# Storing the transposed X and Z from ScalarE's queue, with a third place for the transposed X

## The chip, the cores and the metric

The kernel runs on one core of a Trainium2 chip. Its engines are TensorE (PE in the profile, with its weight loads as PEld), VectorE (DVE), ScalarE (ACT), GpSimd (POOL) and SyncE (SP), which here only issues transfers. All engines work side by side, each in its own fixed order, and meet at semaphores. The metric is the device time of one execution in microseconds (us), as the median of several runs.

## The reference

One inference step of one layer: 512 latent tokens and 128 context tokens of width 2048 go through adaLN modulation, an input projection, a time mixer (RWKV-7, scanned in both directions, 16 heads of 64) beside a chunked gMLP, an output projection and a SwiGLU channel mixer. The part that matters here is the scan:

```python
def step(S, inp):
    r_t, w_t, k_t, v_t, a_t, b_t = inp
    sa = jnp.einsum('bhvk,bhk->bhv', S, a_t)
    S = S * w_t[:, :, None, :] + sa[..., None] * b_t[:, :, None, :] + v_t[..., None] * k_t[:, :, None, :]
    return S, jnp.einsum('bhvk,bhk->bhv', S, r_t)

h = _rmsnorm(x, lp['norm1_g']) * (1.0 + sc1) + sh1
p = h @ lp['w_in']
o_a, s_fin = _rwkv7_bidir(shift_fn(p[..., :C_SHIFT], lp['mu_shift']), s0, lp)
```

All arrays are float32.

## The kernel before

All 640 tokens are kept together, in 10 chunks of 64 (`NCH`, `CH`). The scan is done chunk by chunk in matrix form. It has two stages. In the first, while the input projection runs on TensorE, the operands of every chunk are prepared and stored in a DRAM array `d_S`, one record for each head pair, direction and chunk. In the second stage, the records are read back and the states are carried from chunk to chunk.

**The stage around the change.** The loop over `pieces` runs the input projection: 128 output columns at a time (a block), in four pieces of 512 rows of `w_in`. `split` (L160) loads a piece of weights through SP's queue into one of three buffers `raw`, ACT makes the rounded part `hi` (L167), VectorE the remainder `lo` (L168), and `win` (L183) does three products with them into two halves of a PSUM tile `big`. Weights are loaded two pieces ahead (`LEAD`). A finished block is copied out by ACT (`praw`, L952) and handed to a function for its kind of column: `take_r`, `take_v`, `take_k`, `take_gv`, `take_gu`. These are generators; between the matmuls of `win` the three mixers `mixA`, `mixS` and `mixM` run a bit of them at a time, each `yield` naming a cost. So the program interleaves the projection with the preparation of the scan. The 1 MB loads of `w_mod` (`wt`, L889), with the products `pm` (L900), are strewn in as well. A planner then lays out the order of each engine from estimated times of the instructions and from their dependencies; it also puts in the semaphores. The transfers issued by SP and by ACT share a set of eight semaphores in turn, so a transfer may first wait for an earlier one that used the same semaphore.

**The lines that the change touches** are in `take_k`, which runs once for each of the 8 head pairs and in it twice, once a direction: 16 times, each called a half-pair here. For one half-pair it does the following in this order.

- It makes the decay factors, then R (stored at L622) and X, a tile of 10 chunks. Two loads from `d_vt` (L626) put the values into two blocks of each chunk of the tile Z.
- The products `pG` (L650) give GR (stored at L664, six stores), GA and GB.
- The transposes `pXT` (L668) turn X: first chunks 0 to 7, then chunks 8 and 9, each for two heads h into two PSUM banks. So there are four copies of a PSUM bank into a tile XT by ACT (L674): two of 128x512 and two of 128x128 elements. XT has two places. Each copy is followed by a store to `d_S` (L676): two of 256 KB and two of 64 KB.
- The products `pW` (L682) use the same two PSUM banks, so each bank must have been copied to XT before. ACT copies the four results into the free blocks of Z (L684), and one store of 640 KB brings Z to `d_S` (L686).
- The small blocks of GB go out through GpSimd's queue for the next step, `solve`, and then `merge`, which `mixS` and `mixM` run.

SP's queue is in order: a store at L676 or L686 waits there for ACT's copy, with all later loads and stores behind it. ACT issues only a few transfers: five at the start and, in the second stage, the new states (L1205).

Of the kernel before, what the change touches and what calls it, by code (L numbers as in the profile page):

```python
# [10 lines left out]
F32 = mybir.dt.float32  # L11
# [8 lines left out]
P = 128  # L20
# [5 lines left out]
CH = 64  # L26
# [18 lines left out]
SDIV = 9.0  # L45
HOLD = 68
WAIT = 20
SUBST = 4.6
MODR = 1.36
NREC = 8  # L50
# [34 lines left out]
F_R, F_G, F_X, F_Z, F_T, REC = 0, 128, 256, 384, 512, 576  # L85
# [3 lines left out]
def flow_step(ctx: ExitStack, tc, x_prompt, x_sample, state_rwkv, c, c_ctx, w_mod, b_mod,  # L89
# [3 lines left out]
    nc = tc.nc  # L93
# [59 lines left out]
    d_S = dp.tile([NPAIR, P, 2, NCH, REC], F32, name="d_S")  # L153
# [207 lines left out]
    bk, bp, gs, bz = (hp.enter_context(tc.tile_pool(name=n, bufs=1)) for n in ("bk", "bp", "gs", "bz"))  # L361
# [138 lines left out]
    def both(name):  # L500
        return [pk.tile([P, 512], F32, tag=f"g{h}", name=name) for h in range(2)]

    def in_turn(fns):
        last = None
        for fn in fns:
            if last is None:
                last = fn()
            else:
                with tc.issue_after(last.ins):
                    last = fn()  # L510
# [38 lines left out]
    def take_k(pr, p):  # L549
# [30 lines left out]
        for d in range(2):  # L580
# [5 lines left out]
            for hf in range(2):  # L586
# [6 lines left out]
                for h, dst in enumerate((sg, tha)):  # L593
                    c = 16 * h + 8 * d + p
# [28 lines left out]
            Z = bz.tile([P, NCH, 2, CH], F32, tag="Z", name="Z")  # L623
# [42 lines left out]
            for (c0, c1) in ((0, 8), (8, NCH)):  # L666
                two = [ps.rearrange("p (c t) -> p c t", t=CH) for ps in both("pXT")]
                in_turn([lambda cc=cc, h=h: TE.transpose(  # L668
                    two[h][:, cc - c0, :], X[hsl(h), cc].rearrange("p s t -> p (s t)"), ident[hsl(h), hsl(h)])
                    for cc in range(c0, c1) for h in range(2)])  # L670
                for h in range(2):
                    ps = two[h]
                    XT = bz.tile([P, 8, CH], F32, tag="XT", name="XT", bufs=2)
                    S.copy(XT[:, 0:c1 - c0, :], ps[:, 0:c1 - c0, :])  # L674
                    yield 0.1 * (c1 - c0)
                    nc.sync.dma_start(d_S[p, :, d, c0:c1, F_X + CH * h:F_X + CH * h + CH], XT[:, 0:c1 - c0, :])  # L676
            two = [ps.rearrange("p (c t) -> p c t", t=CH) for ps in both("pW0")]
            for c0 in (0, 5):
                ps = two[c0 // 5][:, 0:5, :]
# [3 lines left out]
                for h in range(2):  # L683
                    S.copy(Z[osl(h), c0:c0 + 5, h, :], ps[osl(h)])  # L684
                yield 1.0
            nc.sync.dma_start(d_S[p, :, d, :, F_Z:F_Z + P], Z.rearrange("p c h v -> p c (h v)"))  # L686
            o.dd[d] = db.tile([8, NCH, 16, 16], F32, tag=f"dd{d}", name="dd")
            for gq in range(8):
                q = gq % 4
# [99 lines left out]
    def solve(p):  # L789
# [4 lines left out]
        for d in range(2):  # L794
            BQ.dma_start(gi[:, d], o.dd[d].rearrange("g c s t -> g c (s t)"))
        yield WAIT
        tc.keep_in_program_order(V.memset(mx2[:, :, 0], 0.0))
# [128 lines left out]
    for p in range(NPAIR):  # L926
        block(P * p, take_r, 2.6, p)
        block(2 * DA + P * p, take_v, 5.1, p)
        block(DA + P * p, take_k, KCOST, p)
        while g < GORD[p]:  # L930
            block(CSH + DA + P * g, take_gv, 12.0, g)
            block(CSH + P * g, take_gu, 5.0, g)
            g += 1
# [21 lines left out]
    def between(k):  # L955
        if k in GRAN:
            f = 1.0 / (2 * len(GRAN))
            mixA.run(f * max(AMIN, 8.0 * mixA.pace()))
            mixS.run(f * SUBST)
            mixM.run(f * max(SMIN, mixM.left / SDIV), k == GRAN[-1])  # L960
# [1158 lines left out]
```

## Time and profile before

| what | us |
|---|---|
| median of 3 runs | 3245.55 |
| range of the runs | 3244.21 to 3252.82 |
| the profiled execution: its time | 3255.98 |
| the profiled execution: its span | 3254.2 |

The span runs from the first to the last instruction of the program; 1.8 us of the profiled execution's time lie outside it. The views used are these. Busy time counts work of an engine; issuing a transfer and waiting for a semaphore are not counted as busy. A row of the waits names who waited, for whom, the total in us, the number of times and (in the list of all waits) the longest. A row of the groups has a line, an engine, an operation, the tiles written and read, the count, busy time and mean duration in ns, and the idle time of the engine ahead of them with what ended it. A row in order of time has a start, a duration and, in brackets, the idle time ahead of it with what ended it. SP's own rows end in q, since all that it does is done by its sequencer; so do ACT's issues. The list by line has the shortest, the median and the longest duration in ns. In the chain of waits, a row that begins with DMA is the time from the issue of a transfer to the wait that it ended.

### The profile page before, as it was taken

What the parts mean: (1) busy time and instruction counts of PE and PEld (TensorE: products, weight loads), DVE (VectorE), ACT (ScalarE), POOL (GpSimd) and SP (SyncE); (2) the same over time, 40 slices, a digit from 0 to 9 for tenths busy, and PEclk for the clock granted to TensorE, in tenths of its full rate; (3) what the DMA queues carried; (4) which work ended last, traced back from release to release, by engine and by line L of the source; (5) the groups of instructions that cost most, each with busy time, mean ns of one, the idle gap of its engine ahead of it and who ended that gap; (6) DMA issues with size and microseconds to landing.
All of it is one profiled execution on the core that took longest, in us unless ns stands there. A gap on an engine that the chain in (4) does not pass through costs nothing.

```text
span 3254.2 us, 72319 instructions
## 1 busy us (share of the span) xinstructions
PE 3113.8 (96%) x28216; PEld 2872.8 (88%) x28216; DVE 2365.7 (73%) x4115; ACT 1459.9 (45%) x3197; POOL 1218.3 (37%) x1065
## 2 busy tenths in 40 slices
PE   6999999999999999999999999999999999999997
PEld 3687778777777888899899999999999999999997
DVE  4548766676676677766878778777777787887788
ACT  3344444454344444345644444444444445443365
POOL 2001121211112113422356655665665645454542
PEclk9999999999999999999999999999999999999999
DMA  9666676777678588654444344344344364553453
GB/s 371 222 197 197 192 217 181 197 205 193 184 194 227 159 275 269 200 173 151 129 130 122 106 129 127 103 128 127 108 124 121 117 189 150 162 155 105 150 165 120
DMA packets 740438, 550.88 MB, mean 169 GB/s; under 512 B 141056, under 2 KB 673504, under 8 KB 731264
## 3 DMA queue, kind: packets, MB, share of 16 engines
q1 hardware_dynamic: 727136, 532.47, 54.2%
q0 software_dynamic: 10624, 13.23, 1.8%
q8 instruction: 222, 3.64, 0.5%
q14 instruction: 120, 0.98, 0.1%
q10 hardware_dynamic: 2336, 0.57, 0.1%
HBM read 437.79 MB, written 110.95 MB: 169 GB/s over the span
## 4 chain that ended last, share of the span: by engine, by line
PE 72%; DVE 10%; DMA 7%; issue 6%; POOL 3%; ACT 2%; SPq 0%; DVEq 0%; POOLq 0%; ACTq 0%
PE P L1637 15%; PE P L1635 15%; PE P L1636 15%; PE big L189 5%; PE big L191 4%; PE big L190 4%; PE pm L900 2%; DMA wt<-in_w_mod_dram 1%; DVE lo L1417 1%; PE pG L650 1%; PE big L1475 1%; PE big L1476 1%; PE big L1477 1%; PE big L1032 1%; DVE mx L803 1%
## 5 line engine op out<-in xcount | busy, mean ns | idle before, releaser
L1637 PE MATMUL P<-xo,lo 128*128 128x320 f32 x2352 | 728.0, 310 | 2.6 <-DVE lo L1417 2.5
L1635 PE MATMUL P<-xo,hi 128*128 128x320 f32 x2352 | 727.4, 309 | 0.7 <-ACT hi L1416 0.7
L1636 PE MATMUL P<-xo,hi 128*128 128x320 f32 x2352 | 727.2, 309 | 0.0
L1417 DVE TENSOR_TENSOR lo<-raw,hi 128x512 fp32r<-128x512 f32 x526 | 499.9, 954 | 178.0 <-ACT hi L1416 172.8
L1416 ACT CAST hi<-raw 128x512 fp32r<-128x512 f32 x526 | 327.0, 622 | 486.0 <-PE P L1636 384.6
L189 PE MATMUL big<-h_hi,hi 128*128 128x320 f32 x1376 | 450.9, 328 | 8.2 <-ACT hi L167 4.8
L1637 PEld LDWEIGHTS P<-xo,lo 128*128 128x128 f32 x2352 | 441.9, 188 | 4.0 <-DVE lo L1417 4.0
L1635 PEld LDWEIGHTS P<-xo,hi 128*128 128x128 f32 x2352 | 441.9, 188 | 1.0 <-ACT hi L1416 1.0
L1636 PEld LDWEIGHTS P<-xo,hi 128*128 128x128 f32 x2352 | 441.9, 188 | 0.0
L191 PE MATMUL big<-h_hi,lo 128*128 128x320 f32 x1376 | 434.2, 316 | 1.1 <-DVE lo L168 0.9
L190 PE MATMUL big<-h_lo,hi 128*128 128x320 f32 x1376 | 433.6, 315 | 0.6 <-DVE h_lo L351 0.6
L1545 POOL TENSOR_TENSOR raw<-raw 128x512 f32<-128x512 f32 x252 | 409.0, 1633 | 16.4 <-DVE lo L1417 4.9
L1637 PE MATMUL P<-xd,lo 128*128 128x320 f32 x1232 | 385.2, 313 | 18.7 <-DVE lo L1417 18.4
L1635 PE MATMUL P<-xd,hi 128*128 128x320 f32 x1232 | 383.1, 311 | 1.5 <-ACT hi L1416 0.6
L1636 PE MATMUL P<-xd,hi 128*128 128x320 f32 x1232 | 382.1, 310 | 0.0
L168 DVE TENSOR_TENSOR lo<-raw,hi 128x512 fp32r<-128x512 f32 x268 | 184.0, 689 | 204.0 <-ACT hi L167 193.6
L189 PEld LDWEIGHTS big<-h_hi,hi 128*128 128x128 f32 x1376 | 262.5, 191 | 76.2 <-issue 50.6
L1416 ACT CAST hi<-rawd 128x512 fp32r<-128x512 f32 (+1 forms) x288 | 168.8, 587 | 243.5 <-PE P L1636 206.4
L191 PEld LDWEIGHTS big<-h_hi,lo 128*128 128x128 f32 x1376 | 262.6, 191 | 10.8 <-issue 3.5
L190 PEld LDWEIGHTS big<-h_lo,hi 128*128 128x128 f32 x1376 | 263.3, 191 | 6.4 <-issue 1.7
L167 ACT CAST hi<-raw 128x512 fp32r<-128x512 f32 x268 | 165.1, 618 | 223.9 <-PE big L190 112.2
L1637 PEld LDWEIGHTS P<-xd,lo 128*128 128x128 f32 x1232 | 232.5, 189 | 25.6 <-DVE lo L1417 25.4
(403 smaller groups left out, 6109.2 us busy)
## 6 DMA issues: line engine op xcount, KB each, us to landing
wt<-in_w_mod_dram SPq DMA_DIRECT2D x96, 1024.0 KB
raw<-in_w_ffn_gate_dram SPq DMA_DIRECT2D x182, 256.0 KB
raw<-in_w_ffn_up_dram SPq DMA_DIRECT2D x182, 256.0 KB
rec<-d_S SPq DMA_DIRECT2D x80, 576.0 KB
raw<-in_w_in_dram SPq DMA_DIRECT2D x172, 256.0 KB
rawd<-in_w_ffn_down_dram SPq DMA_DIRECT2D x128, 256.0 KB
raw<-in_w_out_dram SPq DMA_DIRECT2D x96, 256.0 KB
xd<-d_os SPq DMA_DIRECT2D x66, 320.0 KB
```

The source lines that it names most:

```text
L167: S.copy(hi, raw)
L168: V.tensor_sub(lo, raw, hi.bitcast(F32))
L189: TE.matmul(halves[hf], hi[:, k, :], h_hi[:, kb, s], start=(kb == 0), stop=False)
L190: TE.matmul(halves[hf], hi[:, k, :], h_lo[:, kb, s], start=False, stop=False)
L191: TE.matmul(halves[hf], lo[:, k, :], h_hi[:, kb, s], start=False, stop=(kb == KB - 1))
L900: TE.matmul(pm[32 * j:32 * j + 2, :], cT[:, 2 * kb:2 * kb + 2], quad[:, j, :], start=(kb == 0), stop=(kb == KB - 1), tile_position=(0, 32 ...
L1416: S.copy(hi[:, 0:nk], raw[:, 0:nk])
L1417: V.tensor_sub(lo[:, 0:nk], raw[:, 0:nk], hi[:, 0:nk].bitcast(F32))
L1545: G.tensor_tensor(out=o[:, 0:nk], in0=p[:, 0:nk], in1=q[:, 0:nk], op=ALU.subtract)
L1635: TE.matmul(ps, hi[:, k, :], xk[:, 0, :], start=f, stop=False)
L1636: TE.matmul(ps, hi[:, k, :], xk[:, 1, :], start=False, stop=False)
L1637: TE.matmul(ps, lo[:, k, :], xk[:, 0, :], start=False, stop=l)
```

## The change

The stores of XT and of Z are issued by ACT instead of SP, and XT has three places instead of two. A constant `NW` is added, which nothing uses.

```diff
@@ -45,6 +45,7 @@
 SDIV = 9.0
 HOLD = 68
 WAIT = 20
+NW = 8
 SUBST = 4.6
@@ -670,10 +671,10 @@
                 for h in range(2):
                     ps = two[h]
-                    XT = bz.tile([P, 8, CH], F32, tag="XT", name="XT", bufs=2)
+                    XT = bz.tile([P, 8, CH], F32, tag="XT", name="XT", bufs=3)
                     S.copy(XT[:, 0:c1 - c0, :], ps[:, 0:c1 - c0, :])
                     yield 0.1 * (c1 - c0)
-                    nc.sync.dma_start(d_S[p, :, d, c0:c1, F_X + CH * h:F_X + CH * h + CH], XT[:, 0:c1 - c0, :])
+                    nc.scalar.dma_start(d_S[p, :, d, c0:c1, F_X + CH * h:F_X + CH * h + CH], XT[:, 0:c1 - c0, :])
@@ -683,7 +684,7 @@
                 for h in range(2):
                     S.copy(Z[osl(h), c0:c0 + 5, h, :], ps[osl(h)])
                 yield 1.0
-            nc.sync.dma_start(d_S[p, :, d, :, F_Z:F_Z + P], Z.rearrange("p c h v -> p c (h v)"))
+            nc.scalar.dma_start(d_S[p, :, d, :, F_Z:F_Z + P], Z.rearrange("p c h v -> p c (h v)"))
```

A third place is 2 KB more in each partition of on-chip memory.

## The prediction

> **What bounds the kernel now.** I read the page first, then the busy time in four stretches, then who waited for whom in the one stretch in which the touched lines run, then single stalls in order of time.
>
> ```profile
> span 3254.2 us, 72319 instructions
> PE 3113.8 (96%) x28216; PEld 2872.8 (88%) x28216; DVE 2365.7 (73%) x4115; ACT 1459.9 (45%) x3197; POOL 1218.3 (37%) x1065
> PE 72%; DVE 10%; DMA 7%; issue 6%; POOL 3%; ACT 2%; SPq 0%; DVEq 0%; POOLq 0%; ACTq 0%
> ```
> ```profile
> 0.00:200.00 200.00, 165.59 (x1071) 122.27 (x1072) 95.12 (x207) 70.59 (x113) 19.56 (x37) 0.95 0.79 274
> 200.00:1050.00 850.00, 806.22 (x9477) 669.17 (x9477) 591.65 (x1141) 385.59 (x846) 149.85 (x245) 0.97 0.72 199
> 1050.00:1500.00 450.00, 432.34 (x6127) 386.74 (x6126) 318.47 (x843) 197.84 (x669) 113.14 (x142) 0.99 0.69 213
> 1500.00:3254.20 1754.20, 1709.62 (x11547) 1694.65 (x11545) 1360.49 (x1927) 805.83 (x1569) 935.71 (x642) 0.99 0.43 132
> ```
>
> The columns after the stretch are its length and the busy time of PE, PEld, DVE, ACT and POOL. TensorE sets the time. The edit touches only the stretch from 200 to 1050 us, where the 16 half-pairs (8 head pairs, two directions) are prepared. There TensorE stands idle for 850 - 806.2 = 43.8 us, and ACT is busy for 385.6, or 45%. So the edit can save at most a part of 43.8 us, and what it puts on ACT costs only where TensorE already stands waiting for ACT. The next view says which part that is.
>
> ```profile
> ACT XT L674 <- DMA d_S<-XT: 24.1, 7, 5.9
> ACT hi L167 <- DMA raw<-in_w_in_dram: 11.7, 13, 2.6
> PEld pW L682 <- ACT XT L674: 8.5, 5, 4.8
> PE pW L682 <- ACT XT L674: 7.2, 3, 4.5
> PE pm L900 <- DMA wt<-in_w_mod_dram: 5.5, 4, 2.7
> PEld pXT L668 <- ACT XT L674: 4.6, 12, 1.6
> ```
> ```profile
> L674 ACT COPY XT<-pXT 128x128 f32<-128x128 f32 x32 | 8.3, 260 | 24.6 <-DMA d_S<-XT 24.1
> ```
>
> Total, number, longest. ACT waits 24.1 us, 7 times, for a place of XT to come free, always at the small copies, which are the third and the fourth of a half-pair (the row by shapes); in order of time it is the third each time. TensorE itself waits for XT copies 7.2 us at the product pW, in three places. Weight loads overlap running matmuls, so the matmul rows count. One half-pair in order of time (ACT rows, then the three stalls of TensorE and one product after it):
>
> ```profile
> 640.91 1.06 ACT L674 COPY XT<-pXT 128x512 f32<-128x512 f32 x2
> 647.88 0.27 ACT L674 COPY XT<-pXT 128x128 f32<-128x128 f32 x1 [5.91 <-DMA d_S<-XT]
> 649.80 0.26 ACT L674 COPY XT<-pXT 128x128 f32<-128x128 f32 x1
> 648.20 0.80 PE L682 MATMUL pW<-Z,GA 64*64 64x64 f32 x20 [0.84 <-ACT XT L674]
> 684.95 0.80 PE L682 MATMUL pW<-Z,GA 64*64 64x64 f32 x20 [1.89 <-ACT XT L674]
> 934.59 1.33 PE L682 MATMUL pW<-Z,GA 64*64 64x64 f32 x20 [4.51 <-ACT XT L674]
> 937.48 1.33 PE L682 MATMUL pW<-Z,GA 64*64 64x64 f32 x20
> ```
>
> Copies 1 and 2 fill the two places; copy 3 comes when the first store has landed, here 6 us later; then pW can take its bank. 0.84 + 1.89 + 4.51 = 7.24, the whole of the row above.
>
> How much does ACT's standing still cost TensorE? I cut out the seven waits of copy 3 exactly (first, longest, and their sum):
>
> ```profile
> 231.33:234.91 3.58, 3.58 (x26) 3.46 (x26) 0.69 (x1) 0.00 (x1) 0.15 (x1) 1.00 1.06 295
> 641.97:647.88 5.91, 5.39 (x36) 4.87 (x35) 0.00 (x0) 0.01 (x1) 0.23 (x1) 1.00 0.86 240
> sum 24.14, PE 23.16 PEld 19.70 DVE 1.09 ACT 0.02 POOL 2.27; mean PE 3.31 PEld 2.81 DVE 0.16 ACT 0.00 POOL 0.32
> ```
>
> While ACT does nothing for 24.14 us, TensorE is busy for 23.16. A microsecond in which ACT stands costs 0.98 / 24.14 = 0.04 us of TensorE's time. That ratio limits both the gain and the loss.
>
> **The change, part by part.** The stores and what they cost on the queue that has them now:
>
> ```profile
> L676 SPq DMA_DIRECT2D d_S<-XT x64: 359/363/1603, 230.3 to 1027.4; - x64
> L676 SPq EVENT_SEMAPHORE  x55: 17/17/17, 229.1 to 1025.1; - x55
> L686 SPq DMA_DIRECT2D d_S<-Z x16: 359/363/1275, 240.2 to 1030.1; - x16
> L1205 ACTq DMA_DIRECT2D out_dram<-ST x8: 378/417/476, 1182.8 to 1389.5; - x8
> SPq L676 <- ACT XT L674: 64.4, 36, 6.4
> SPq L686 <- ACT Z L684: 20.4, 12, 4.0
> SPq L166 <- DVE lo L168: 212.6, 107, 8.8
> ```
>
> *Issues moved to ACT.* 64 + 16 = 80 issues leave SyncE (SP) and go to ACT, at 0.363 us there; the one store that ACT issues already (L1205) takes 0.417. Does an issue hold ACT's engine? The only place that shows it:
>
> ```profile
> 1182.77 0.44 ACTq L1205 DMA_DIRECT2D out_dram<-ST  x1
> 1182.82 0.19 ACT L1132 ACTIVATION_READ_ACCUMULATOR Y<-y_ps 128x1 f32 x1
> 1182.92 0.21 ACT L1132 ACTIVATE Y<-y_ps 128x64 f32<-128x64 f32 x1
> ```
>
> Here ACT went on computing beside the issue, because that store waits for VectorE. The stores of XT and Z wait for ACT's own copy, so nothing of ACT is left in flight and the next copy begins only after the issue. I take 0.42 us of standing for each, 80 x 0.42 = 33.6 us in all, on an engine that is idle 55% of the stretch. Exposed at the ratio of 0.04 that is 1.3 us. The lower bound is 0 (all issues fall in idle time). The upper one: behind a store stand the second copy of each pair, for which the transposes of the last chunks wait (12 times the weight load already stands there, 4.6 us), the fourth copy, for which the second pW waits, and after Z the next evacuation: 3 x 16 x 0.42 = 20 us. I take +2, near the row of the ratio.
>
> *Waits moved to ACT.* Ahead of 55 of the 64 XT stores, SP carries a further wait for an earlier transfer that uses the same semaphore. All lasted 17 ns, so they were over when SP came; on ACT I put 0 for them. Were one not over, the casts of weights (hi) and all evacuations would queue behind it.
>
> *Waits and issues off SP.* SP loses 80 x 0.363 = 29 us of issues (at the median) and 64.4 + 20.4 = 84.8 us of standing for ACT's copies, which held the weight loads behind them. But the loads mostly wait for a free buffer (212.6 us), and TensorE has no stall for them among its matmul rows except 5.5 us for wt. The longest of these, 2.7 us, ended with a load that took 9.26 us to land, so it was a late landing and not a late issue:
>
> ```profile
> 836.86 9.26 DMA wt<-in_w_mod_dram
> ```
>
> Bounds -5.5 and 0; a load let go earlier can also run into the stores, which the landing rows would show and no row prices. I take -0.5.
>
> *The third place.* It removes the wait of copy 3 for the first store. Copy 4 then waits for that store, where it now waits for the second. So the 24.1 us do not vanish: part moves to copy 4. The first pW is freed (-7.24 at best); the second pW, which now follows 2.9 us after the first (934.59 and 937.48), may stall in its place. In the 4.51 and the 1.89 us stalls copy 3 stood behind other ACT work, and copy 4 could come to stand there. Bounds -7.2 and 0; I take the middle, -4, for want of a row that decides.
>
> How late the first store lands decides what copy 4 still waits:
>
> ```profile
> 641.51 6.27 DMA d_S<-XT
> ```
>
> In the kernel before, 6.27 us from issue to release in the worst case, in one ring with 256 KB and 1 MB loads. The Trainium skill, page "DMA: Bandwidth & Descriptors", section "Queues, rings and completion order", says that a DMA engine takes the queues that have work in turn, packet by packet; by that the store would overtake SP's loads and copy 4 would wait hardly at all, and the third place would give its full -7.2. The same page's section "Issuing engines are not separate DMA queues" says that issuing from several engines saves only the sequencer's time to issue; by that the landing stays as it is and the sum would be that of my middle value or worse. No row of the kernel before decides between them.
>
> *Order.* A planner lays out each engine's order from estimated times, so work beside the stores can change places. Nothing in the trace prices that. The stretch has 43.8 / 16 = 2.7 us of idle TensorE time in a half-pair; I let a quarter of all of it, 11 us, come or go for the range.
>
> Sum: +2 + 0 - 0.5 - 4 = -2.5 us, against the profiled span of 3254.2. The unprofiled median is 3245.55, and the difference carries over: 3243. A difference under 0.3%, 9.7 us, I call no change; that is about what three runs, 3244.21 to 3252.82, can tell.
>
> **Rivals.** *Slower: issues between the copies.* Each store put between two evacuations makes TensorE wait for the second: the 20 us of the upper bound, less at most 4 from the third place, +16: 3262. For it: TensorE's weight loads already stand at these copies 12 times. Against it: the seven windows, in which ACT stood far longer than 0.42 us and TensorE lost 4%. It decides if the planner puts the issue ahead of the second copy, and if the slack at these points is under 0.42 us. Chance 0.17.
>
> *Faster: stores land early on their own ring.* Neither copy 3 nor copy 4 waits: -7.2, and SP, freed of 84.8 us, brings wt in time: -5.5, with issues hidden: -12.7, 3233. For it: the 6.27 us landing behind loads. Against it: it needs every stall of both rows to go, and the wt stalls are not at an XT store. Chance 0.15.
>
> *Nothing: the wait only moves.* Copy 4 takes copy 3's wait, the second pW the first one's stall, and the third place gives 0: +2 - 0.5, 3247. Chance 0.18.
>
> **How the numbers follow.** The forecast, 3243, has 0.50. With reordering of 11 us either way its own range is 3232 to 3254. The slower rival draws the upper end to 3258; at the lower end 3232 holds the faster one. About 0.1 is left out on each side. Faster by over 0.3%: the 0.15 and a little of the forecast's edge, 0.18. Slower: 0.17 and the same, 0.18. Within 0.3%: 0.64.
>
> **What would show it.** In the changed profile: 80 issues of about 0.4 us on ACT and none on SP; the wait of XT for its store far below 24.1 us, or moved to the fourth copy; pW's wait for XT copies (7.2) at 3 or less; the second transposes' wait for XT copies up by less than 3 us; TensorE's idle time of 43.8 us in the stretch changed by under 10. The slower rival shows as more idle time before pXT and pW that XT copies end, the faster one as the loss of both that and the wt wait. I am wrong if issues on ACT last over 1 us, if a semaphore wait ahead of them lasts microseconds, or if the stretches after 1050 us change.

## The result, and the profile after

| what | before | after |
|---|---|---|
| median, four runs each (us) | 3245.10 | 3273.65 |
| range of the runs (us) | 3244.21 to 3252.82 | 3267.75 to 3277.16 |
| the profiled execution: time (us) | 3255.98 | 3267.75 |
| the profiled execution: span (us) | 3254.2 | 3266.0 |

The change makes the kernel slower: ratio 1.0081 [1.0060, 1.0102] (in brackets the 95% interval). The two profiled executions show only 11.8 us of the 28.5 us between the medians, because the one of before was slower than all four of its kernel's runs and the one of after is the fastest of its four. All lines of the changed kernel from the copy of XT on bear a number one higher.

The page of the changed kernel: the span, the busy time of the engines, ACT's transfer queue (packets, MB, share of 16 engines) and the shares of the chain that ended last.

```profile
span 3266.0 us, 72293 instructions
...
PE 3108.7 (95%) x28216; PEld 2864.2 (88%) x28216; DVE 2358.8 (72%) x4115; ACT 1463.9 (45%) x3197; POOL 1225.1 (38%) x1065
...
q10 hardware_dynamic: 65056, 21.54, 2.6%
...
PE 69%; DVE 11%; DMA 8%; issue 6%; ACT 3%; POOL 3%; SPq 0%; ACTq 0%; DVEq 0%; POOLq 0%
```

TensorE is busy for no longer than before (3113.8 there), so the time was lost as idle time. ACT's queue carries 21.54 MB, where it carried 0.57. The four stretches, with the columns of before (PE, PEld, DVE, ACT, POOL, then the granted clock):

```profile
0.00:200.00 200.00, 165.87 (x1077) 122.14 (x1078) 96.23 (x207) 70.72 (x113) 19.55 (x37) 0.94 0.79 274
200.00:1050.00 850.00, 784.72 (x9163) 646.96 (x9161) 569.08 (x1111) 379.46 (x827) 145.38 (x241) 0.97 0.70 193
1050.00:1500.00 450.00, 431.22 (x6302) 383.45 (x6302) 319.54 (x845) 194.47 (x665) 113.04 (x143) 0.99 0.72 218
1500.00:3266.00 1766.00, 1726.90 (x11680) 1711.61 (x11678) 1373.93 (x1955) 819.23 (x1594) 947.10 (x646) 1.00 0.44 133
```

In the stretch with the stores TensorE stands idle for 850 - 784.72 = 65.3 us, 21.5 more than the 43.8 of before, at the same granted clock (0.97). It does 9163 products there instead of 9477; the others slip into the later stretches, so in the last one TensorE is busy for 17.3 us longer (1726.90 against 1709.62). The line of the XT stores, and the waits from 200 to 1080 us (total, times, longest; the last row is of before):

```profile
L677 ACTq DMA_DIRECT2D d_S<-XT x64: 366/427/1736, 229.8 to 1039.4; - x64
L677 ACTq EVENT_SEMAPHORE  x56: 17/17/17, 230.3 to 1039.4; - x56
```
```profile
ACT XT L675 <- DMA d_S<-XT: 45.2, 14, 5.5
PEld pW L683 <- ACT XT L675: 9.5, 8, 2.5
PE pW L683 <- ACT XT L675: 8.3, 7, 2.4
PE pm L901 <- DMA wt<-in_w_mod_dram: 14.8, 7, 5.5
PE pG L651 <- DVE GA L661: 12.0, 10, 2.6
```
```profile
PE pG L650 <- DVE GA L660: 3.4, 5, 1.4
```

All 64 stores are on ACT, at 0.427 us in the median, and the semaphore waits ahead of 56 of them were over when ACT came (17 ns each). But ACT now waits for a place of XT 14 times and 45.2 us in all, where it waited 7 times and 24.1 us. pW's wait for the copies of XT rose only from 7.2 to 8.3. Most of the 21.5 us is elsewhere: the wait of the products pm for wt rose from 5.5 to 14.8, and that of the products pG for GA, which VectorE writes, from 3.4 to 12.0.

One half-pair of the changed kernel in order of time, ACT, then the two products pW, then the first store in the chain of waits:

```profile
652.56 1.07 ACT L675 COPY XT<-pXT 128x512 f32<-128x512 f32 x2
653.17 1.27 ACTq L677 DMA_DIRECT2D d_S<-XT  x2
655.82 0.27 ACT L675 COPY XT<-pXT 128x128 f32<-128x128 f32 x1 [2.19 <-PE pXT L669]
660.77 0.27 ACT L675 COPY XT<-pXT 128x128 f32<-128x128 f32 x1 [4.68 <-DMA d_S<-XT]
660.85 0.89 ACTq L677 DMA_DIRECT2D d_S<-XT  x2
661.83 0.42 ACT L685 COPY Z<-pW 64x320 f32<-64x320 f32 x1 [0.80 <-ACT XT L675]
```
```profile
659.19 0.80 PE L683 MATMUL pW<-Z,GA 64*64 64x64 f32 x20
661.09 0.80 PE L683 MATMUL pW<-Z,GA 64*64 64x64 f32 x20 [1.10 <-ACT XT L675]
```
```profile
653.17 7.51 DMA d_S<-XT
```

Copy 3 gets the third place as soon as its transposes are done (655.82). Copy 4 follows it directly in ACT's order and stands for 4.68 us, until the first store has landed, 7.51 us after its issue (the row of the chain). Stores 3 and 4 are both issued behind copy 4, and Z's first copy begins when their issues are over. In the kernel before, ACT had other work in this place. I counted in both traces what ACT runs between the copies of the 16 half-pairs: before, 0 to 6 other instructions between copies 2 and 3 and 1 to 4 between 3 and 4; after, none in any of the 16. So the planner, which laid other work into the time of the landing in the kernel before, lays none there in the changed one.

The 14 waits cut out exactly (first, longest, and the sum of all):

```profile
231.46:236.95 5.49, 3.73 (x41) 3.41 (x39) 0.00 (x0) 0.00 (x0) 0.55 (x1) 1.00 1.04 289
...
821.20:826.61 5.41, 3.37 (x37) 2.99 (x37) 0.64 (x2) 0.01 (x2) 0.54 (x1) 1.00 0.89 238
...
sum 45.16, PE 37.98 PEld 31.62 DVE 4.65 ACT 0.02 POOL 5.39; mean PE 2.71 PEld 2.26 DVE 0.33 ACT 0.00 POOL 0.39
```

TensorE stands for 45.16 - 37.98 = 7.2 us of them, 16%, against 4% of the seven waits of before. The single waits are no longer (45.16 / 14 = 3.2 us in the mean, against 24.14 / 7 = 3.4), but TensorE ran out of work in seven of the 14, where it did so in two of the seven. What is held up on ACT behind the wait comes on top of that and isn't in these windows.

### The profile page after: what moved, and what is told of

Its sections match the earlier page's. It is cut to its first block, busy times and chain, and to the rows that moved or that the text cites. A ratio compares the mean times of both kernels' runs of the same rounds, so it can differ in the third digit from the quotient of the medians.

```text
span 3266.0 us, 72293 instructions
## 1 busy us (share of the span) xinstructions
PE 3108.7 (95%) x28216; PEld 2864.2 (88%) x28216; DVE 2358.8 (72%) x4115; ACT 1463.9 (45%) x3197; POOL 1225.1 (38%) x1065
## 3 DMA queue, kind: packets, MB, share of 16 engines
q10 hardware_dynamic: 65056, 21.54, 2.6%
## 4 chain that ended last, share of the span: by engine, by line
PE 69%; DVE 11%; DMA 8%; issue 6%; ACT 3%; POOL 3%; SPq 0%; ACTq 0%; DVEq 0%; POOLq 0%
PE P L1638 15%; PE P L1636 15%; PE P L1637 15%; PE big L190 4%; PE big L192 3%; PE big L191 3%; DMA wt<-in_w_mod_dram 2%; DMA d_S<-GR 2%; DVE lo L1418 1%; PE pm L901 1%; DMA d_S<-XT 1%; DVE mx L804 1%; PE big L1476 1%; PE big L1478 1%; PE big L1477 1%
```

## The experiments

Two causes lie in one edit: the stores go another way, and the planner lays a new order, in which, by the names in the profile, 462 of ACT's 3197 instructions and 3319 of TensorE's 28216 stand at another place, all of them behind the first store of XT. So beside the parts of the change there are kernels in which only a number that the planner's interleaving reads is altered. In the expectations of e1 to e12, A is the theory that ACT's queue holds up ACT, B that the planner's new order costs the time, C that transfers land late. Ratios are to the kernel before in the same series, with their 95% intervals.

**The parts one by one.** In e1 only the third place, in e2 only XT's stores on ACT, in e3 only Z's, in e4 both with two places.

```diff
-XT = bz.tile([P, 8, CH], F32, tag="XT", name="XT", bufs=2)
+XT = bz.tile([P, 8, CH], F32, tag="XT", name="XT", bufs=3)
```
```diff
-nc.sync.dma_start(d_S[p, :, d, c0:c1, F_X + CH * h:F_X + CH * h + CH], XT[:, 0:c1 - c0, :])
+nc.scalar.dma_start(d_S[p, :, d, c0:c1, F_X + CH * h:F_X + CH * h + CH], XT[:, 0:c1 - c0, :])
```
```diff
-nc.sync.dma_start(d_S[p, :, d, :, F_Z:F_Z + P], Z.rearrange("p c h v -> p c (h v)"))
+nc.scalar.dma_start(d_S[p, :, d, :, F_Z:F_Z + P], Z.rearrange("p c h v -> p c (h v)"))
```

The first block is e1, the second e2, the third e3, the second and third together e4.

> Both stores stay on SP, XT has three places. Three theories stand. (A) ScalarE's queue: in the changed kernel ACT stood 45.2 us at the fourth copy, with everything behind it, and the stores on ACT make this worse; the third place alone is then harmless or good, 3238 to 3246. (B) The planner's order: any edit that changes an estimated time lays out TensorE's order anew, and the +28 us are where the stalls happened to fall; then this edit too moves the time, by up to 20 us and with either sign. (C) Transfers: XT stores on ACT's queue land later (the first of a half-pair after 5.1 us on the mean instead of 4.1) and hold SP by the shared semaphores, so that wt comes late; nothing of it happens here: 3241 to 3249, and the wait of pm for wt stays near 5.5 us.

> XT's stores alone go to ACT, with two places as before; Z's store stays on SP. (A) 64 of the 80 issues are on ACT and the third copy waits in ACT's queue: most of the loss is here, 3262 to 3275. (B) Anything from 3235 to 3275, with no tie to the wait of ACT at XT. (C) Most of the loss is here, with the wait of pm for wt at 10 us or more.

> Z's store alone goes to ACT: 16 issues of 0.37 us. (A) At most 16 x 0.37 = 6 us: 3245 to 3251. (B) Not tied to that bound: 3235 to 3275. (C) Z's stores are few; 3243 to 3249, wt wait near 5.5 us.

> Both stores on ACT, XT with two places: the whole change without the third place. (A) As slow as the changed kernel or slower, 3268 to 3285, with ACT's wait for XT at 45 us or more. (B) Unrelated to the sum of the parts. (C) As slow as the changed kernel, 3265 to 3280, the wait of pm for wt at about 15 us.

| kernel | median us | ratio |
|---|---|---|
| e1, third place, SP's queue | 3253.27 | 1.0028 [1.0015, 1.0041] |
| e2, XT on ACT, two places | 3276.75 | 1.0091 [1.0075, 1.0107] |
| e3, Z on ACT | 3258.77 | 1.0043 [1.0027, 1.0059] |
| e4, both on ACT, two places | 3265.51 | 1.0065 [1.0053, 1.0077] |

Waits of e1, then of e2, then of e4:

```profile
ACT XT L674 <- DMA d_S<-XT: 2.9, 2, 1.8
PE pW L682 <- ACT XT L674: 0.6, 1, 0.6
```
```profile
ACT XT L674 <- DMA d_S<-XT: 43.7, 17, 7.3
PE pW L682 <- ACT XT L674: 11.1, 9, 2.3
```
```profile
ACT XT L674 <- DMA d_S<-XT: 53.8, 19, 7.7
PE pW L682 <- ACT XT L674: 13.9, 9, 3.7
```

The third place does on SP's queue what the change was thought to do: ACT's wait falls from 24.1 to 2.9 us, pW's from 7.2 to 0.6. Yet the kernel is slower. The move to ACT's queue does the reverse: with two places ACT waits 43.7 us in e2 and 53.8 in e4, at copy 3 in 30 of the 36 cases, where the six kernels with two places on SP's queue have 18.2 to 29.5. So it is the move that lengthened the wait; in the change the third place took 53.8 - 45.2 = 8.6 us off it again, and the wait now stands at copy 4. In e2 and e4 ACT has 1 to 3 other instructions between copies 3 and 4, by my count, so the copies stand close together only with the stores on ACT and three places or more. e3 lies above what A allowed (3251). Every part costs, and they don't add up (e2 alone costs more than e4, which holds it; their mean granted clocks are 0.982 and 0.985). So something other than the stalls at XT moves the time by ten microseconds.

**The planner's order alone, and four places.** e5 to e7 and e12 leave the stores as they are; each alters one number of the program's interleaving. e8 is the change with four places.

```diff
# e5
-yield 0.1 * (c1 - c0)
+yield 0.11 * (c1 - c0)
# e6
-WAIT = 20
+WAIT = 21
# e7, after the copies of Z
-yield 1.0
+yield 1.05
# e12
-KCOST = 50.0
+KCOST = 50.5
# e8, with both stores on ACT
-XT = bz.tile([P, 8, CH], F32, tag="XT", name="XT", bufs=3)
+XT = bz.tile([P, 8, CH], F32, tag="XT", name="XT", bufs=4)
```

> Nothing of the stores is changed: SP's queue, two places. Only the cost named by the yield after a copy of XT goes from 0.1 to 0.11 a chunk, which shifts a little what the program interleaves and so what the planner lays out. (A) and (C), the cost lies in what ACT and the transfers must do: 3242 to 3249, as before. (B) the cost is that of any new order: 3250 to 3275.

> Again nothing of the stores is changed; the solve of a pair holds back for 21 products instead of 20 (WAIT). (A), (C): 3242 to 3249. (B): 3250 to 3275.

> Again nothing of the stores is changed; the yield after the copies of Z names 1.05 instead of 1.0. (A), (C): 3242 to 3249. (B): 3250 to 3275. If the three kernels without a change of stores spread as widely as the four with one (3253 to 3277), no part of the change has a price of its own that these times can show.

> The whole change with four places for XT instead of three, so that no copy of a half-pair waits for a store of the same half-pair. ACT's wait of 45.2 us for the places should fall under 10. (A) The stall at the fourth copy is the cost: 3245 to 3255. (B) The wait goes and the time does not follow: 3250 to 3280, with stalls elsewhere. (C) The late landings stay: 3262 to 3275.

| kernel | median us | ratio |
|---|---|---|
| e5, XT's yield | 3251.46 | 1.0025 [1.0013, 1.0036] |
| e6, WAIT | 3251.51 | 1.0021 [1.0008, 1.0033] |
| e7, Z's yield | 3266.55 | 1.0072 [1.0053, 1.0090] |
| e8, the change with four places | 3264.13 | 1.0063 [1.0044, 1.0082] |

A number that moves no store costs 7 to 22 us (the medians less the 3244.82 of before in that series). In e8, ACT's wait for a place is gone, and the time hardly better than that of the change (A had put it at 3245 to 3255). One order of each kind could not part the two causes, so the kinds were put into more orders.

**The change in other orders.** e9, e10 and e11 are the full change with the edits of e5, e6 and e7; e12 is the fourth order without it.

> The whole change together with the shifted yield of the fifth run (3251.5 alone, before 3245): the pair shows what the change adds to another order. (A), (C), stores on ACT cost 28 us of their own: about 3280. (B), nothing but a new order: around 3258, the mean of the four kernels with SP's stores, with a spread of 10 either way; the pair's difference may have either sign.

> The whole change with WAIT 21 (3251.5 alone). (A), (C): about 3280. (B): 3245 to 3270, not tied to its pair.

> The whole change with the shifted yield after Z's copies (3266.6 alone). (A), (C): about 3295. (B): 3245 to 3270, and likelier below its pair than above, since 3266.6 is the slowest order without a change of stores.

> Nothing of the stores is changed; the cost that the program names for a block of k is 50.5 instead of 50. (A), (C): 3242 to 3249. (B): 3250 to 3270. Were it at 3245 or below, the order of the kernel before would be no lucky one, and (B) would have to explain why three others were slower.

| kernel | median us | ratio |
|---|---|---|
| e9, the change and XT's yield | 3267.18 | 1.0077 [1.0059, 1.0095] |
| e10, the change and WAIT | 3267.46 | 1.0070 [1.0054, 1.0086] |
| e11, the change and Z's yield | 3270.82 | 1.0085 [1.0071, 1.0099] |
| e12, KCOST | 3262.45 | 1.0052 [1.0036, 1.0068] |

If the change cost nothing of its own, its four orders would scatter as the others do. They lie together, at 1.0070 to 1.0085, and each is above its partner without the change. A and C, which had put e9 to e11 at 3280 to 3295, were too high: the price on top of the order is below the 28 us that the plain pair showed, 0.0013 to 0.0052, or 4 to 17 us, in these three.

**Four places in those orders.** This tells ACT's wait for a place from the issue on ACT's queue: four places take the wait away and leave the issue. e13 to e15 and e17 are e9 to e11 and e16 with `bufs=4`; e16 is the change with e12's constant; e18 is the third place alone, stores on SP's queue, with e12's constant.

```diff
# e16: the change, and
-KCOST = 50.0
+KCOST = 50.5
# e13 (of e9), e14 (of e10), e15 (of e11), e17 (of e16)
-XT = bz.tile([P, 8, CH], F32, tag="XT", name="XT", bufs=3)
+XT = bz.tile([P, 8, CH], F32, tag="XT", name="XT", bufs=4)
# e18: of e16, both stores as before
-nc.scalar.dma_start(d_S
+nc.sync.dma_start(d_S
```

> Stores on ScalarE's queue with four places for XT, and the yield after the copy of XT 0.11 instead of 0.1 a chunk. So far, over four orders each, orders without any change of the stores cost a mean of 1.0043 and the full change 1.0078, so about 1.0035 (11 us) belongs to the change itself. (P) That price is ScalarE's longer wait for a place of XT (49.7 against 25 us in the profiles) and what it brings to pW: with four places it is gone, and the ratio is that of the same yield without the change, 1.0025, about 3253 us. (Q) The price is the issue on ScalarE's queue whatever the places: as the full change with this yield, 1.0077, about 3270. (R) There is no price, only the spread of orders: anywhere between 1.002 and 1.009, without regard to the group.

> The same four places on ScalarE's queue, with WAIT = 21. (P) as the order alone, 1.0021, about 3252 us; ScalarE's wait for stores of XT at zero to 4 us. (Q) as the full change with this wait, 1.0070, about 3268. (R) anywhere between 1.002 and 1.009.

> The same four places on ScalarE's queue, with 1.05 instead of 1.0 after the copies of Z. (P) as the order alone, 1.0072, about 3268 us. (Q) as the full change with this yield, 1.0085, about 3273. (R) anywhere between 1.002 and 1.009. This run alone hardly tells P from Q; it counts for the mean of the group of four, which P puts at 1.0045 with the earlier run of four places (1.0063) and Q at 1.0074.

> The full change (three places, both stores on ScalarE's queue) with KCOST 50.5 instead of 50; without the change this constant cost 1.0052. A price of the change itself (P and Q) of 0.0035 puts it at 1.0087 or, as the other four of its group, at 1.0070 to 1.0085, about 3268 to 3273 us. (R) anywhere between 1.002 and 1.009; below 1.005 would take the change's own price away.

> Stores on ScalarE's queue, four places, KCOST 50.5. The same constant cost 1.0119 in the full change with three places and 1.0052 with nothing of the stores changed. If ScalarE's wait for a place of XT (56.7 us with three places) is the price of the change, it falls to under 5 us and the ratio to that of the order alone or a little below, 1.003 to 1.006, about 3258 to 3267 us. If the issue on ScalarE's queue is the price, it stays at 1.009 to 1.012, 3277 to 3287 us.

> The third place alone, stores on SyncE's queue as before, KCOST 50.5. Against the full change with this constant (1.0119) only the queue differs. If three places suffice when the stores are SyncE's, as the wait of 2.9 us in the earlier run of the third place says, ScalarE waits under 8 us for a store and the ratio is at or a little below that of the order alone (1.0052): 1.003 to 1.006, 3258 to 3267 us. If the third place itself makes an order that costs more, it is over 1.008, 3274 us.

| altered number | stores as before | third place, SP | the change (3 places, ACT) | four places, ACT |
|---|---|---|---|---|
| none | 1 | 1.0028 | 1.0081 [1.0060, 1.0102] | 1.0063 [1.0044, 1.0082] |
| XT's yield | 1.0025 | | 1.0077 [1.0059, 1.0095] | 1.0019 [1.0007, 1.0031] |
| WAIT | 1.0021 | | 1.0070 [1.0054, 1.0086] | 1.0021 [1.0010, 1.0033] |
| Z's yield | 1.0072 | | 1.0085 [1.0071, 1.0099] | 1.0030 [1.0016, 1.0045] |
| KCOST | 1.0052 | 1.0064 [1.0045, 1.0084] | 1.0119 [1.0103, 1.0135] | 1.0092 [1.0068, 1.0117] |
| mean of five | 1.0034 | | 1.0086 | 1.0045 |

(Medians: e13 3255.31, e14 3255.90, e15 3258.06, e16 3289.31, e17 3276.47, e18 3264.86 us.) The change is above the stores as before in all five rows, by 0.0013 to 0.0081, in the mean by 0.0052 or 17 us. The fourth place, with every store still on ACT, brings it down in all five rows, by 0.0018 to 0.0058, in the mean by 0.0041 or 13 us. From the spread of the five differences I estimate 95% intervals of 7 to 27 us for the first and 6 to 21 us for the second. SP's queue instead of ACT's, with three places, brings it down by 0.0053 and 0.0055 in the two rows that have it. Rows share an altered number and not the whole order, so a single difference means little; the sign in all rows does. Not everything went as expected: in the first and the last row the fourth place returns only 6 and 9 us, and e17 stands at 1.0092, where the wait alone as the cause would have had it at 1.003 to 1.006.

The granted clock is a rival for a part of this. Its mean over the runs is 0.987 in the kernel before, 0.984 in the change, 0.982 in e16 and e17, 0.986 to 0.987 in e13 to e15. Among the runs of one kernel, 0.001 less goes with some 2 us more. If that held between kernels, the price of the change and the share of the fourth place would each be about a fifth smaller, an estimate, with the same sign in all five rows. Whether an order lowers the clock or the clock was lower by chance, no run shows.

What the fourth place takes away is the wait. Waits of e16, e17 and e18, the same constant in each:

```profile
ACT XT L674 <- DMA d_S<-XT: 56.7, 16, 5.7
PE pW L682 <- ACT XT L674: 7.1, 6, 2.2
PE pm L900 <- DMA wt<-in_w_mod_dram: 22.8, 8, 5.1
```
```profile
ACT Z L684 <- PE pW L682: 64.8, 16, 7.3
PE pm L900 <- DMA wt<-in_w_mod_dram: 23.5, 10, 5.8
```
```profile
ACT XT L674 <- DMA d_S<-XT: 3.4, 2, 2.4
PE pW L682 <- ACT XT L674: 1.1, 1, 1.1
PE pm L900 <- DMA wt<-in_w_mod_dram: 12.8, 7, 3.4
```

e17 has no row in which XT waits for a store or pW for XT. ACT still stands, for pW (64.8 us, where e16 has 16.9), but these waits end with work of TensorE's own. The busy time from 200 to 1050 us in e16, e17 and e18, then in e9 and e13:

```profile
200.00:1050.00 850.00, 777.64 (x8696) 642.01 (x8695) 558.75 (x1075) 368.04 (x803) 139.25 (x232) 0.96 0.69 189
```
```profile
200.00:1050.00 850.00, 787.02 (x9037) 653.99 (x9035) 570.67 (x1104) 373.57 (x822) 144.28 (x240) 0.96 0.71 192
```
```profile
200.00:1050.00 850.00, 808.20 (x9369) 660.73 (x9369) 589.34 (x1134) 385.87 (x839) 145.87 (x242) 0.97 0.73 196
```
```profile
200.00:1050.00 850.00, 790.53 (x9123) 651.20 (x9124) 569.95 (x1114) 378.23 (x826) 145.29 (x240) 0.97 0.70 193
```
```profile
200.00:1050.00 850.00, 799.15 (x9335) 659.49 (x9333) 582.84 (x1136) 382.68 (x839) 147.13 (x242) 0.97 0.71 197
```

TensorE's idle time: 72.4 us with three places on ACT, 63.0 with four, 41.8 with three on SP; 59.5 and 50.9 in the other pair. The means of all five rows, from one profiled execution of each kernel (waits from 200 to 1080 us):

| mean of the five rows (us) | stores as before | the change | four places, ACT |
|---|---|---|---|
| ACT's wait for a place of XT | 25.1 | 51.1 | none |
| pW's wait for copies of XT | 4.6 | 9.1 | none |
| pm's wait for wt | 9.3 | 14.6 | 15.6 |
| pG's wait for GA | 4.8 | 8.0 | 7.9 |
| TensorE's idle time, 200 to 1050 us | 46.9 | 62.1 | 55.8 |

The change raises TensorE's idle time in all five rows, by 4.8 to 25.2 us. The fourth place lowers it in four of them, by 7.0 to 9.4 us, but not with WAIT (53.9 and 55.0). In the mean it returns 6.3 of the 15.2 us, and pW's wait goes whole. The waits for wt and for GA, together some 9 us above those of the stores as before, stay with four places. So the wait for a place is shown as one part of the price; by the times it is the larger part, by TensorE's idle time the smaller.

Why three places are enough on SP's queue shows in ACT's order again. This is the half-pair of e18 at about the same time:

```profile
645.13 1.07 ACT L674 COPY XT<-pXT 128x512 f32<-128x512 f32 x2 [1.18 <-PE pXT L668]
647.15 0.27 ACT L674 COPY XT<-pXT 128x128 f32<-128x128 f32 x1 [0.94 <-PE pXT L668]
648.89 0.85 ACT L684 COPY Z<-pW 64x320 f32<-64x320 f32 x2 [1.48 <-PE pW L682]
649.64 0.62 ACT L167 CAST hi<-raw 128x512 fp32r<-128x512 f32 x1
651.22 0.53 ACT L595 ACTIVATE sg<-pwa,w0h 128x320 f32<-128x320 f32 x1 [0.96 <-PE pwa L592]
651.64 0.26 ACT L674 COPY XT<-pXT 128x128 f32<-128x128 f32 x1
```

Copy 4 comes 4.5 us after copy 3, and Z's first two copies, a cast of weights and more are done in between; it then waits for nothing. By my count there are 3 to 8 other instructions of ACT between copies 3 and 4 in e1 and e18, and none in e16 and e17. In e17 the fourth place takes the wait for a store out of the same tight order.

**What stays open.** With four places on ACT the mean is 0.0011 above the stores as before, with rows from -0.0042 to +0.0063: that is no measured price, and bounds the issues on ACT only loosely. The wait for wt is large in e16 and e17 alike (22.8 and 23.5 us) and 12.8 in e18; whether it, and pG's wait for GA, belong to the queue or to the order wasn't tried. Nor was it tried why the planner sets the four copies together when ACT issues the stores and XT has three places or more. What an order that moves no store pays its 7 to 22 us for is open as well: in e5 to e7 and e12 TensorE's idle time in the stretch is 46.8 to 49.1 us, only 3 to 5 above that of before. No version beats the kernel before; the nearest is e13, at 1.0019 [1.0007, 1.0031].

## Why the prediction was wrong

The forecast was 3243, the range ended at 3258, and 3273.65 was measured. The step that failed is the move of the issues to ACT, priced at +2 for the time of the 80 issues alone, together with the third place, priced at -4 with bounds of -7.2 and 0. Both were read from the order of the old trace, in which copy 4 has other work ahead of it. The prediction said itself that copy 4 would then wait for the first store, and gave a rival to it ("the wait only moves"), but it did not foresee that the move makes the wait longer. With the stores on ACT and two places ACT waits 53.8 us; with three, copy 4 stands right behind copy 3 and it still waits 45.2, where only a part of the 24.1 was to be left. On SP's queue the third place did take the wait away (2.9 us). In the two rows in which only the queue differs, the move costs 0.0053 and 0.0055, some 17 us, against the +1.5 of the sum's terms for the move (+2, 0 and -0.5). By the five orders the price of the whole change is some 17 us as well, of which a fourth place returns some 13 by the times; how much of the rest is the waits for wt and GA, and from where they come, stays open. The other 11 us of the 28 are the order of before.

- *Issues moved to ACT, +2.* The count (64 + 16) and the time (0.427 us against 0.42 assumed) were right. So was it that an issue holds what stands behind it: in the changed kernel no instruction of ACT begins while one of the 80 issues runs. But the planner put the issues of stores 1 and 2 behind copy 2 in all 16 half-pairs, and those of stores 3 and 4 behind copy 4, ahead of Z's copies. So the slower rival's mechanism, issues between the copies, did not come about, though a slower result did.
- *Semaphore waits on ACT, 0.* Right: 17 ns each.
- *Relief of SP, -0.5.* There was none to see. wt's stall rose from 5.5 to 14.8 us in the changed kernel; in the orders without the change it isn't fixed either (5.5 to 11.6).
- *The ratio of 0.04* "limits both the gain and the loss". It was read from waits of before, whose cover the old order had provided. In the changed kernel it is 0.16 inside the waits, and the 51.1 us that a fourth place removes in the mean of five rows return 6.3 us of TensorE, 0.12 (from none with WAIT to 0.18). One of the seven waits of before, the 0.45 us at 590.05, was copy 4's and not copy 3's. A ratio of cover holds for the order from which it was read.
- *Order, 11 us either way.* Mis-sized and wrong in its symmetry. Orders that change no store cost +7 to +22 us, and none gained: the order of before is a favourable one among the five, by luck or by earlier tuning. The mean of the change over its five orders, 0.0086 above the kernel before, is 0.0052 of the change's own and 0.0034, or 11 us, by which the order of before is better than the mean of its five.
- *What would show it.* The wait did move to the fourth copy, but without falling. TensorE's idle time was to change by under 10 us and rose by 21.5; pW's wait went up instead of to 3 or less. The weight loads of the second transposes waited less for XT copies (3.1 us against 4.6), which speaks against the slower rival too. The stretches after 1050 us kept their rates and only took over late work.
- *Stores landing early on their own ring* (the faster rival). They land later. From the semaphore events of the 16 half-pairs, the first store lands 4.1 us after its issue in the mean before (SP) and 5.1 us after the change; it is 4.0 to 4.4 us in the eight kernels with XT's stores on SP and 4.8 to 5.6 in the twelve with them on ACT. The Trainium skill, page "DMA: Bandwidth & Descriptors", section "Queues, rings and completion order", says that an engine takes the queues with work in turn. From this the prediction inferred that an own ring overtakes the loads, and these landings do not bear that out. The same page's section "Issuing engines are not separate DMA queues" of the Trainium skill says that issuing from several engines saves only the sequencer's time to issue. That is nearer to what the trace shows.

## What to carry to other kernels

Where a planner lays out the order, an edit's stalls can't be read from the old order: ask what will stand next to the moved instruction, and count the instructions between a buffer's release and its next use after the change. Before a difference under 1% is put down to an edit, alter a number that should do nothing and see how far the time moves; here that was up to 22 us, of the size of the effect. A further buffer helps only if it covers the whole landing in the new order: three places were enough for SP's stores, four for ACT's.

## What the runs showed of the hardware

- An issue of an XT store takes 0.427 us of ACT's sequencer in the median of the changed kernel. The kernels differ in this: 0.366 us (e2) to 0.513 (e13) on ACT, and 0.360 (e5) to 0.452 (e18) on SP, so these runs show no price of the one queue over the other.
- In the changed kernel no instruction of ACT begins while one of the 80 issues of XT and Z runs, though one that stands ahead of it may still run (in the half-pair shown the issue starts at 653.17, and copy 2 ends at 652.56 + 1.07 = 653.63). At the eight stores of the states it is otherwise: in seven of them an instruction of ACT begins during the issue. Why, no run shows.
- A queue of its own didn't bring the stores in sooner: 4.8 to 5.6 us after the issue, as the mean of a kernel, against 4.0 to 4.4 on SP's, and 7.51 in the half-pair shown.
- SP came to wait for stores that ACT had issued. Waits of SP in the changed kernel (the first), and of before (the second):

```profile
SPq L627 <- DMA d_S<-Z: 38.2, 6, 11.4
SPq L890 <- DMA d_S<-XT: 18.1, 3, 6.1
```
```profile
SPq L626 <- DMA d_S<-Z: 9.6, 5, 3.3
```

The loads into Z stand for the store of Z four times as long as before. The loads of wt stand three times for a store of XT, with which they share no buffer; the semaphores that both queues take in turn are the likely link, though no run took them apart. Such rows stand in all ten kernels with both stores on ACT and three or four places, e13 and e14 among them, which cost no more than their orders; so these waits alone don't set the time there, but moving a store to another queue did not free SP from it.
